# Where the later modulation columns are computed: from attention to the values' stage and retention, with retention's state steps widened and its normed result on ScalarE

## The chip, the cores and the metric

One Trainium2 chip, one of its cores. The metric is the device time of one execution in microseconds (us), the median of the runs shown. The core has a matrix engine (PE, TensorE), three elementwise engines (DVE is VectorE, ACT is ScalarE, POOL is GpSimd), and SP (SyncE), which here only issues DMA transfers. SBUF is the memory of 128 partitions that the engines work on, and PSUM holds PE's results in eight banks of 512 numbers for each partition.

## The reference

A decoder block on 1024 tokens of 1024 channels, all float32. A vector c gives six modulation vectors, `mod = silu(c) @ w_ada + b_ada`: shift, scale and gate of the token mixer (sh1, sc1, g1) and of the MLP (sh2, sc2, g2).

```
h = modulate(rms_norm(x, norm1_g), sh1, sc1)
x = x + g1 * token_mixer(h)
h = modulate(rms_norm(x, norm2_g), sh2, sc2)
x = x + g2 * square(relu(h @ w1)) @ w2
out = rms_norm(x, norm_f_g)
```

The token mixer adds two gated branches. One is retention: 4 heads, 256 channels of queries and keys, 512 of values, in 8 chunks of 128 tokens.

```
s = (q @ k.T) * inner_decay
o = s @ v + (q @ state) * q_decay
state = state * chunk_decay + (k * k_decay).T @ v
```

Each row of o is then normalised (its mean taken off, divided by the root of variance plus 1e-5), scaled, shifted, multiplied by silu(rg) and projected. The other branch is dilated window attention in three groups of four heads, whose results are merged by their softmax denominators.

## The kernel before

Every product of float32 matrices is made of three matmuls on rounded operands: each operand x is split into a high part (a rounded copy, by ScalarE) and a low part (x minus the high part, by DVE), and `mm3` (L199 to L206) adds low times high, high times low and high times high. L202, L204 and L206 are therefore the lines of nearly all matmuls, and L192 and L193 those of the splits of weights (`split_w`).

The stages follow each other in time: attention's values, queries and keys (`queries_keys`), retention's values (`values`), retention (`chunk`, 32 times), attention (`att_step`, `cover_step`, `gate_step`), the output projections, the MLP.

All instructions stand in the order in which the program writes them; each engine works through its own list in that order and waits at an instruction until its operands are there. So the place of a line decides what stands behind it.

`Steps` runs the program as a list of steps, each with its loads and a body. Loads go through one ring (`raw`) of three buffers, issued on SP in the order of the list, never more than three ahead of those used (L85 is the issue). Before a body runs, all loads of the next step are prepared, and those loads at the head of the step after it that are weights. Preparing a weight is its split; preparing queries (`q_prep`, L1210 and L1211) is theirs; preparing a modulation column (`mod_prep`, L453 to L455) is one DVE product with the silu of c (`cb`, broadcast over the partitions) that also sums, and a small addition of the bias. Of the 48 columns of 128 numbers, 16 are made at the start. The other 32 (`later_mods`) are loads of later steps: three in each head of retention (ahead of chunks 2, 5 and 7), and 20 in attention, two for each of ten steps.

**Values.** `values` goes through 14 items (`VSEQ`), each with four parts of 12 matmuls (`v_mm`). Weight loads are issued two items ahead; high and low parts of the next item (`v_w`, `v_low`) are made in parts 0 to 2, results of the part before are handled after each part (`v_post`). The table of cosines, `cs`, was used for the rotations in the stage before, and is not read here.

**Retention.** `chunk(h, c)` writes, in this order: PE's product of keys and values for the new state (kv, two banks), a part of the projection of rg; DVE's update of the state, by 512 columns twice (L700, L702); the preparing of the next step's load (`ahead(2)`); the scores of the next chunk (`s_kt`: sT and kT on PE, then sm, smh, sml, kh, kl on ScalarE and DVE, L636 to L647); o on PE; the high and low parts of the state, by 512 columns twice (L715, L716); the next-but-one chunk's queries (`jit_qk`: j on ScalarE, its low part on POOL); the transposes of the previous chunk's normed result (`on_T`: oT on PE, four copies on ScalarE); the rest of rg; mean and variance of o (L726, L727), gr, the reciprocal root on POOL (L729), a multiply (L730), and the normed result onm on DVE (L732). In four chunks of each head after the first, `u_final` follows: scale and shift on ScalarE (L668, two halves), the product with silu(rg) on DVE (L670), and the store of y. PSUM has, in retention, two pairs of banks (tag mm, `ps_mm`) and four single banks (tag s, `ps_s`).

**Attention.** `att_step` projects one head's keys (ak, 48 matmuls), with the scores of the previous head woven in after two of eight parts; then splits the keys (`k_split`: kh on ScalarE L1219, kl on DVE L1220), and takes maximum and exponential of the previous head's scores (`scores_end`). There are six such steps for each of two pairs of heads. In the first step, POOL's queue is given the sums of y in DRAM (`result_sums`).

Of the kernel before, what the change touches and what calls it, by code (L numbers as in the profile page):

```python
# [40 lines left out]
CS_QD = 132  # L41
CS_QD2 = 136
# [92 lines left out]
def block_kernel(ctx, tc, io, stop=None, dbg=None):  # L135
# [37 lines left out]
    cb = cst.tile([P, 1024], F32, name="cb")  # L173
# [141 lines left out]
    right0 = r0.enter_context(tc.tile_pool(name="right0", bufs=1, side="right"))  # L315

# [355 lines left out]

    def chunk(h, c, ahead, w=None):
# [15 lines left out]
        kvs = []  # L689
        if c < NC - 1:  # L690
            kh, kl = hd["k", g]
            for i in range(2):
                kv = ps_s(f"kv{h}{c}{i}")
                mm3([kv], (kh[:, i, :], kl[:, i, :]), [(vh, vl)], True, True)
                kvs.append(kv)
        if g > 0:
            proj_mm(hd["rgp"], hd["rgw"], ks[:1])
        for i, kv in enumerate(kvs):
            if c == 0:
                nc.vector.tensor_copy(st[:, i, :], kv)  # L700
            else:
                nc.vector.scalar_tensor_tensor(st[:, i, :], st[:, i, :], float(GAMMA[h] ** C), kv,  # L702
                                               op0=ALU.mult, op1=ALU.add)
        ahead(2)
        if g + 1 < NG:
            s_kt(g + 1)
        po = ps_s(f"o{h}{c}")
# [5 lines left out]
        if c < NC - 1:  # L713
            for i in range(2):
                nc.scalar.copy(sh[:, i, :], st[:, i, :])  # L715
                nc.vector.tensor_sub(sl[:, i, :], st[:, i, :], fv(sh[:, i, :]))  # L716
# [11 lines left out]
        nc.vector.tensor_scalar(gr, ba[:, 1:2], ct[:, CS_QD2 + h:CS_QD2 + h + 1], GN_EPS, op0=ALU.mult, op1=ALU.add)  # L728
        nc.gpsimd.tensor_tensor(gr, gr, mhalf[:, 0:1], op=ALU.pow)  # L729
        nc.vector.tensor_mul(gr, gr, ct[:, CS_QD + h:CS_QD + h + 1])  # L730
        on = p.tile([P, DV], F32, tag="on", bufs=1, name=f"onm{h}{c}")
        nc.vector.tensor_scalar(on, po, ba[:, 0:1], gr, op0=ALU.subtract, op1=ALU.mult)  # L732
        hd["o", h, c] = on
# [335 lines left out]

    def values(ahead):  # L1070
# [3 lines left out]
        for i, (hp, n) in enumerate(VSEQ):  # L1074
            if i + 2 <= last:
                v_load(i + 2)
            for p in range(4):
# [8 lines left out]
                if p == 2 and i < last:  # L1086
                    v_low(i + 1, 1)

# [21 lines left out]
    for g in (1, 2):  # L1110
        for kk in range(4):
# [4 lines left out]
    later_mods = [G1 + k for k in range(NK)] + [SH2 + k for k in range(NK)] + \  # L1116
                 [SC2 + k for k in range(NK)] + [G2 + k for k in range(NK)]
# [216 lines left out]
    def weights(pair):  # L1334
# [4 lines left out]
        wt = p.tile([P, 3, 8, 2], F32, tag="wt", name=f"wt{pair}")  # L1339
        wg = p.tile([P, 2, 8, 2], F32, tag="wg", name=f"wg{pair}")  # L1340
# [8 lines left out]
        nc.vector.tensor_add(sm, stn[0][:, :, 2:4], stn[1][:, :, 2:4])  # L1349
        nc.vector.tensor_add(sm, sm, stn[2][:, :, 2:4])  # L1350
# [121 lines left out]
    def att_step(pair, i):  # L1472
# [3 lines left out]
        def body(*args):  # L1476
# [897 lines left out]
def _constants():  # L2374
# [9 lines left out]
    for h in range(H):  # L2384
# [4 lines left out]
        cst[:, CS_QD + h] = np.exp(lg * (i + 1))  # L2389
        cst[:, CS_QD2 + h] = np.exp(2 * lg * (i + 1))  # L2390
# [71 lines left out]
```

## Time and profile before

| | us |
|---|---|
| median of three runs | 2323.57 (2323.11 to 2323.8) |
| the profiled execution | 2327.32 |
| its span, first to last instruction | 2325.5 |
| PE busy | 2198.7 (95%) |
| DVE busy | 1486.2 (64%) |
| ACT busy | 920.8 (40%) |
| POOL busy | 145.2 (6%) |

Times in the trace count from the first instruction. A line of the kernel is named L and its number. In a group row stand the number of instructions, then the engine's busy time in us and the mean of one in ns, then the idle time of the engine just before them and what ended it. In a wait row stand who waited, for whom, the total in us, how often, and the longest. Durations of PE's matmuls overlap: 128 x 512 matmuls start some 0.23 us apart and last 0.39. The granted clock is a share of full speed.

### The profile page before, as it was taken

Reading aid. Unit: us, or ns where it says so; the run is one execution under the profiler, and the core shown is the slowest. Engines: PE = TensorE matmul, PEld = TensorE weight load, DVE = VectorE, ACT = ScalarE, POOL = GpSimd, SP = SyncE. Lnnn points to the kernel's source line nnn. Section 1 sums busy time; section 2 is a strip of 40 time slices with the busy share of each in tenths; the row PEclk is TensorE's granted clock in tenths of the full one; section 3 lists DMA queues with packets and bytes.
Section 4 is the critical chain, followed back from the end, with each engine's and each line's share of the span. In section 5 each row is a group of like instructions: output and inputs, shape, how many; then the busy total and the mean of one; then the engine's idle time right before and its main releaser. Section 6 shows DMA issues by size and latency. Waiting matters only on the chain.

```text
span 2325.5 us, 27170 instructions
## 1 busy us (share of the span) xinstructions
PE 2198.7 (95%) x10082; PEld 1813.7 (78%) x10082; DVE 1486.2 (64%) x2341; ACT 920.8 (40%) x1697; POOL 145.2 (6%) x168
## 2 busy tenths in 40 slices
PE   7999999999999998875989999999989999999998
PEld 5877888888787777764877878888868888788887
DVE  6537777764445888853555564486786665687845
ACT  4423222332343545532543543534454444443412
POOL 0001111000001222200000000001100000000003
PEclk9999999999999999987999999999999999999999
DMA  9548998432477465478433336555224443745322
GB/s 357 204 144 295 280 299 253 155 127 91 181 253 250 158 208 186 159 253 235 143 108 100 110 125 229 208 199 195 95 94 155 150 150 121 290 164 179 118 84 73
DMA packets 156674, 417.30 MB, mean 179 GB/s; under 512 B 27318, under 2 KB 55229, under 8 KB 152126
## 3 DMA queue, kind: packets, MB, share of 16 engines
q1 hardware_dynamic: 150846, 371.53, 45.5%
q0 software_dynamic: 5696, 44.04, 8.0%
q8 instruction: 79, 1.29, 0.2%
q14 instruction: 53, 0.43, 0.1%
HBM read 320.46 MB, written 160.32 MB: 207 GB/s over the span
## 4 chain that ended last, share of the span: by engine, by line
PE 44%; DVE 6%; DMA 4%; ACT 3%; issue 1%; POOL 0%; SPq 0%; POOLq 0%; DVEq 0%; ACTq 0%
PE fp L202 4%; PE fp L204 4%; PE fp L206 4%; DMA raw<-in_w_ak_dram 2%; PE f2a L204 2%; PE f2a L206 2%; PE f2a L202 2%; ACT P L1273 1%; PE wo L202 1%; PE wo L204 1%; PE wo L206 1%; PE roa L206 1%; PE roa L204 1%; PE roa L202 1%; PE ak L202 1%; PE ak L204 1%
## 5 line engine op out<-in xcount | busy, mean ns | idle before, releaser
L202 PE MATMUL qap<-hh,qaw 128*128 128x512 f32 x264 | 102.9, 390 | 3.9 <-ACT qat L281 2.2
L204 PE MATMUL qap<-hl,qaw 128*128 128x512 f32 x264 | 102.7, 389 | 0.0
L206 PE MATMUL qap<-hh,qaw 128*128 128x512 f32 x264 | 102.7, 389 | 0.0
L614 POOL TENSOR_TENSOR j<-qk,j 128x512 fp32r<-128x512 f32 x32 | 43.1, 1348 | 490.9 <-ACT j L613 490.9
L1919 ACT ACTIVATE a<-a 128x512 f32<-128x512 f32 x48 | 30.3, 632 | 78.7 <-DVE a L1918 78.7
L202 PEld LDWEIGHTS qap<-hh,qaw 128*128 128x128 f32 x264 | 49.5, 188 | 15.0 <-ACT qat L281 2.6
L1273 ACT ACTIVATE P<-P,ng 128x128 f32<-128x128 f32 (+1 forms) x96 | 41.9, 438 | 45.1 <-DVE ng L1270 45.1
L202 PE MATMUL sc<-kh,ql 128*128 128x256 f32 (+1 forms) x96 | 28.3, 295 | 33.2 <-ACT kh L1219 33.2
L206 PEld LDWEIGHTS qap<-hh,qaw 128*128 128x128 f32 x264 | 49.5, 188 | 10.3
L204 PEld LDWEIGHTS qap<-hl,qaw 128*128 128x128 f32 x264 | 49.6, 188 | 10.2
L259 DVE TENSOR_TENSOR fw<-w1r,fw 128x512 fp32r<-128x512 f32 x48 | 33.0, 688 | 36.3 <-ACT fw L249 36.3
L1816 POOL TENSOR_TENSOR accnf<-accnf,sqnf 128x256 f32<-128x256 f32 (+1 forms) x18 | 16.6, 921 | 619.9 <-ACT sqnf L1815 619.9
L259 DVE TENSOR_TENSOR qaw<-wa,qaw 128x512 fp32r<-128x512 f32 x66 | 45.1, 687 | 14.9 <-ACT qaw L249 14.5
L2105 ACT CAST w2h<-w2s 128x512 fp32r<-128x512 f32 x36 | 22.4, 621 | 78.0 <-DVE w2s L2143 76.2
L202 PE MATMUL fp<-h2h,fw 128*128 128x512 f32 x128 | 50.0, 391 | 0.0
L1816 POOL TENSOR_TENSOR accn<-accn,sqn 128x512 f32<-128x512 f32 x12 | 15.6, 1297 | 549.8 <-ACT sqn L1815 549.8
L206 PE MATMUL fp<-h2h,fw 128*128 128x512 f32 x128 | 49.8, 389 | 0.0
L204 PE MATMUL fp<-h2l,fw 128*128 128x512 f32 x128 | 49.8, 389 | 0.0
L202 PE MATMUL roa<-rh,rwl 128*128 128x512 f32 x128 | 49.8, 389 | 0.0
L204 PE MATMUL roa<-rl,rwh 128*128 128x512 f32 x128 | 49.8, 389 | 0.0
L206 PE MATMUL roa<-rh,rwh 128*128 128x512 f32 x128 | 49.8, 389 | 0.0
L249 ACT CAST qaw<-wa 128x512 fp32r<-128x512 f32 x66 | 39.7, 617 | 24.9 <-PE qap L206 22.3
(3073 smaller groups left out, 7161.3 us busy)
## 6 DMA issues: line engine op xcount, KB each, us to landing
v<-vd SPq DMA_DIRECT2D x32, 512.0 KB, 4.9
raw<-in_w_ada_dram SPq DMA_DIRECT2D x32, 512.0 KB, 5.4
w1r<-in_w_ff_dram SPq DMA_DIRECT2D x32, 512.0 KB, 4.9
vd<-vo SPq DMA_DIRECT2D x24, 512.0 KB, 6.5
yt<-y POOLq DMA_DIRECT2D x6, 2048.0 KB, 15.5
xsd<-as SPq DMA_DIRECT2D x24, 512.0 KB, 2.7
w2r<-in_w_ff2s_dram SPq DMA_DIRECT2D x24, 512.0 KB, 7.4
em<-in_w_ada_dram SPq DMA_DIRECT2D x16, 512.0 KB, 10.2
```

The source lines that it names most:

```text
L202: nc.tensor.matmul(o, wl, xh, start=first, stop=False, skip_group_check=skip)
L204: nc.tensor.matmul(o, wh, xl, start=False, stop=False, skip_group_check=skip)
L206: nc.tensor.matmul(o, wh, xh, start=False, stop=last, skip_group_check=skip)
L249: nc.scalar.copy(t[:, :512], src)
L259: nc.vector.tensor_sub(t[:, 512:], src, fv(t[:, :512]))
L614: nc.gpsimd.tensor_sub(t[:, 1], src, fv(t[:, 0]))
L1273: nc.scalar.activation(v, v, AF.Exp, bias=ng[:, blk:blk + 1], accum_out=st[:, g, blk, 2 + a:3 + a])
L1816: (nc.vector if f == 7 else nc.gpsimd).tensor_add(G["acc", key], G["acc", key], sq)
L1919: nc.scalar.activation(o, o, AF.Relu)
L2105: nc.scalar.copy(hi, src)
```

## The change

The 32 later columns are given out anew. Thirteen go to the values' stage: at the start of each item but the last, one column's load is issued on SP into one half of `cs`; `v_mod` makes its sum on DVE in the last part of the item after. The other 19 go to retention: five in heads 0 to 2 (ahead of chunks 1, 2, 3, 5 and 6), four in head 3 (1, 3, 5 and 6). Attention's steps have none.

In `chunk`, kv becomes one pair of banks (`ps_mm`) in place of two single ones; the update of the state, its high part and its low part are each one instruction of 1024 columns. The scale by the query decay is folded into eps: gr becomes one addition ahead of POOL's root, and the multiply after it goes. The normed result is no longer made at the end of the chunk by DVE but by `normed(g - 1)` in the next chunk, behind `s_kt` and ahead of o: a small DVE product (nb, minus mean times gr), and one ScalarE instruction with scale and bias over 512 columns. For the last chunk, `normed` is called in attention's first step.

`cb` moves to a pool that closes after retention, and `weights` writes products and their sum to tiles of their own.

```diff
-CS_QD = 132
-CS_QD2 = 136
+CS_EPS = 132
...
-    cb = cst.tile([P, 1024], F32, name="cb")
...
+    cb = right0.tile([P, 1024], F32, name="cb")
...
+    def normed(g):
+
+        h, c = divmod(g, NC)
+        po, ba, gr = hd["o", h, c]
+        nb = R["p"].tile([P, 1], F32, tag="nb", bufs=2, name=f"nb{h}{c}")
+        nc.vector.scalar_tensor_tensor(nb, ba[:, 0:1], -1.0, gr, op0=ALU.mult, op1=ALU.mult)
+        on = R["p"].tile([P, DV], F32, tag="on", bufs=1, name=f"onm{h}{c}")
+        nc.scalar.activation(on, po, AF.Identity, scale=gr, bias=nb)
+        hd["o", h, c] = on
...
-        kvs = []
         if c < NC - 1:
             kh, kl = hd["k", g]
+            kv = ps_mm(f"kv{h}{c}")
             for i in range(2):
-                kv = ps_s(f"kv{h}{c}{i}")
-                mm3([kv], (kh[:, i, :], kl[:, i, :]), [(vh, vl)], True, True)
-                kvs.append(kv)
+                mm3([kv[:, i]], (kh[:, i, :], kl[:, i, :]), [(vh, vl)], True, True)
...
-        for i, kv in enumerate(kvs):
-            if c == 0:
-                nc.vector.tensor_copy(st[:, i, :], kv)
-            else:
-                nc.vector.scalar_tensor_tensor(st[:, i, :], st[:, i, :], float(GAMMA[h] ** C), kv,
-                                               op0=ALU.mult, op1=ALU.add)
+        if c == 0:
+            nc.vector.tensor_copy(flat(st), flat(kv))
+        elif c < NC - 1:
+            nc.vector.scalar_tensor_tensor(flat(st), flat(st), float(GAMMA[h] ** C), flat(kv),
+                                           op0=ALU.mult, op1=ALU.add)
         ahead(2)
         if g + 1 < NG:
             s_kt(g + 1)
+        if g > 0:
+            normed(g - 1)
         po = ps_s(f"o{h}{c}")
...
-            for i in range(2):
-                nc.scalar.copy(sh[:, i, :], st[:, i, :])
-                nc.vector.tensor_sub(sl[:, i, :], st[:, i, :], fv(sh[:, i, :]))
+            nc.scalar.copy(flat(sh), flat(st))
+            nc.vector.tensor_sub(flat(sl), flat(st), fv(flat(sh)))
...
-        nc.vector.tensor_scalar(gr, ba[:, 1:2], ct[:, CS_QD2 + h:CS_QD2 + h + 1], GN_EPS, op0=ALU.mult, op1=ALU.add)
+        nc.vector.tensor_add(gr, ba[:, 1:2], ct[:, CS_EPS + h:CS_EPS + h + 1])
         nc.gpsimd.tensor_tensor(gr, gr, mhalf[:, 0:1], op=ALU.pow)
-        nc.vector.tensor_mul(gr, gr, ct[:, CS_QD + h:CS_QD + h + 1])
-        on = p.tile([P, DV], F32, tag="on", bufs=1, name=f"onm{h}{c}")
-        nc.vector.tensor_scalar(on, po, ba[:, 0:1], gr, op0=ALU.subtract, op1=ALU.mult)
-        hd["o", h, c] = on
+        hd["o", h, c] = po, ba, gr
...
+    def v_mod(i):
+
+        t, j = cs[:, i % 2], VMODS[i]
+        nc.vector.scalar_tensor_tensor(t, t, 1.0, cb, op0=ALU.mult, op1=ALU.mult, accum_out=mods[:, j:j + 1])
+        nc.vector.tensor_add(mods[:, j:j + 1], mods[:, j:j + 1], vec[:, VC_BADA + j:VC_BADA + j + 1])
+
+    VMODS = [later_mods.pop(0) for _ in range(len(VSEQ) - 1)]
...
+            if i < last:
+                nc.sync.dma_start(cs[:, i % 2], io["w_ada"][VMODS[i]])
...
+                if p == 3 and i > 0:
+                    v_mod(i - 1)
...
-                      ([mod_load(later_mods.pop(0))] if c in (2, 5, 7) else []), manual=True)
+                      ([mod_load(later_mods.pop(0))] if c in ((1, 2, 3, 5, 6) if h < 3 else (1, 3, 5, 6)) else []), manual=True)
...
-            nc.vector.tensor_mul(stn[g][:, :, 2:4], wt[:, g], stn[g][:, :, 2:4])
-        sm = mx
+            nc.vector.tensor_mul(pr[:, g], wt[:, g], stn[g][:, :, 2:4])
...
+                normed(NG - 1)
                 on_T(H - 1, NC - 1)
...
-                      ([(aq_d[pair, *combos[i - 1]], q_prep(pair, *combos[i - 1]))] if i > 0 else []) +
-                      [mod_load(later_mods.pop(0)) for _ in range(2 if i > 0 else 0)],
+                      ([(aq_d[pair, *combos[i - 1]], q_prep(pair, *combos[i - 1]))] if i > 0 else []),
...
-        cst[:, CS_QD + h] = np.exp(lg * (i + 1))
-        cst[:, CS_QD2 + h] = np.exp(2 * lg * (i + 1))
+        cst[:, CS_EPS + h] = GN_EPS * np.exp(-2 * lg * (i + 1))
```

More of the change, by code (lines that the diff above doesn't have):

```diff
@@ L1068, in v_post @@
         nc.sync.dma_start(v_d[2 * hp + int(blk[0]) - 1][:, p + 4 * (int(blk[1]) - 1)], fv(t))
+    later_mods = [G1 + k for k in range(NK)] + [SH2 + k for k in range(NK)] + \
+                 [SC2 + k for k in range(NK)] + [G2 + k for k in range(NK)]
+    def v_mod(i):
[3 more added lines that the diff above has]
+    VMODS = [later_mods.pop(0) for _ in range(len(VSEQ) - 1)]
     def values(ahead):
@@ L1339, in weights @@
         wt = p.tile([P, 3, 8, 2], F32, tag="wt", name=f"wt{pair}")
+        pr = p.tile([P, 3, 8, 2], F32, tag="pr", name=f"pr{pair}")
+        sm = p.tile([P, 8, 2], F32, tag="ssum", name=f"ssum{pair}")
         wg = p.tile([P, 2, 8, 2], F32, tag="wg", name=f"wg{pair}")
@@ L1346, in weights @@
         for g in range(3):
[L1347 to L1350 removed]
+            nc.vector.tensor_mul(pr[:, g], wt[:, g], stn[g][:, :, 2:4])
+        nc.vector.tensor_add(sm, pr[:, 0], pr[:, 1])
+        nc.vector.tensor_add(sm, sm, pr[:, 2])
         nc.vector.reciprocal(sm, sm)
```

2 lines of the change are left out of this document (removed).

## The prediction, made before the changed kernel was run

> **What bounds the kernel now.** The page comes first: which engine is full, and in which slices it isn't. Each row is the span in 40 slices of 58 us, busy share or granted clock in tenths.
>
> ```profile
> PE 7999999999999998875989999999989999999998
> PEclk9999999999999999987999999999999999999999
> ```
>
> PE is full except at the ends and in slices 15 to 20 and 29, and two slices lose clock. So a gain can only come from those places, and a loss is made wherever PE gets a new wait. Next, the busy time by stage: values (579 to 742 us), retention (742 to 996), attention (996 to 1387).
>
> ```profile
> core 0: us, PE busy (x) PEld busy (x) DVE busy (x) ACT busy (x) POOL busy (x), PEclk, DMA share, GB/s
> 579.00:742.00 163.00, 159.22 (x705) 131.41 (x704) 75.84 (x91) 62.79 (x90) 7.09 (x10) 1.00 0.64 223
> 742.00:996.00 254.00, 232.09 (x1111) 187.12 (x1110) 207.61 (x444) 125.44 (x339) 57.08 (x61) 0.98 0.54 178
> 996.00:1387.00 391.00, 327.98 (x1698) 277.03 (x1698) 203.80 (x337) 158.52 (x360) 7.47 (x9) 0.91 0.51 155
> ```
>
> PE is idle 3.8 us in values, 21.9 in retention, 63.0 in attention. Attention also has a mean clock of 0.91; retention has DVE busy for 82% of its time. Then PE's own waits (total, times, longest), first attention, then retention.
>
> ```profile
> PE sc L202 <- ACT kh L1219: 33.2, 4, 15.2
> PE sc L204 <- DVE kl L1220: 14.7, 6, 3.0
> PE pv L1408 <- DVE vl L1303: 5.7, 1, 5.7
> ```
>
> ```profile
> PE o L202 <- DVE state L702: 12.9, 17, 1.3
> PE kT L632 <- DVE onm L732: 6.7, 13, 0.9
> ```
>
> The chain of waits tells why kh is late in attention (start, duration, what).
>
> ```profile
> 1012.32 10.05 DMA raw<-aqd
> 1022.40 1.07 ACT qh L1210
> ...
> 1024.74 11.91 DMA raw<-in_w_ak_dram
> 1036.74 1.05 ACT raw_8204h L192
> ...
> 1086.87 10.33 DMA raw<-in_w_ak_dram
> ```
>
> kh is no slow operation. ScalarE works its list in the order in which it is written, and ahead of kh stands the split of a later step's key weights, whose load has not landed. That load is late because the ring has three raw buffers and a step of attention takes four loads: key weights, queries, two modulation columns. A key weight's buffer comes free only when the step before has used its queries (the load starts at 1024.74, just behind the queries), and then it takes 10 to 12 us.
>
> **Attention loses its 20 columns.** A step is left with two loads. With three buffers, the key weights two steps ahead are then issued while this step begins, a whole step (11 us of projection and the scores) before the split. Loads of 10 to 12 us fit. Gone are the 33.2; most of the 14.7, where kl stands behind two columns on DVE; and the 5.7, where vl does: 53.6 at most. With the waits goes clock. 9% of 391 us is 35 us of clock, which is 70 us at half rate; I take half of them as PE's idle time, where a low clock costs nothing, so 17 us are lost by busy PE. Sum 71. What is late next in the first pair of heads is DMA itself, since the result sums run there on POOL's queue. The same view of the stage, cut finer:
>
> ```profile
> 1038.00:1064.00 26.00, 16.21 (x72) 13.25 (x72) 10.14 (x16) 8.07 (x21) 1.71 (x2) 0.83 0.90 271
> 1064.00:1099.00 35.00, 16.78 (x72) 13.95 (x72) 10.08 (x16) 6.72 (x20) 2.82 (x3) 0.70 0.85 244
> ```
>
> I leave 3 us for it: -68. Bounds: -75 (other small waits go too) and -25 (DMA share stays at 0.9, and loads that are issued earlier also land later). I take the end near -71, since ten of the loads in that queue are gone.
>
> **Values get 13 columns.** Each is one 512 KB load on SP's queue into the table of cosines, idle by then, and the DVE product with its sum, read out and added to the bias. The groups of DVE in retention (count | busy, mean ns | idle before) give their price, and that of what goes there:
>
> ```profile
> L732 DVE TENSOR_SCALAR onm<-o,ba,gr 128x512 f32<-128x512 f32 x31 | 25.1, 811 | 3.6 <-PE kv L206 0.5
> ...
> L453 DVE SCALAR_TENSOR_TENSOR raw<-raw,cb 128x1024 f32<-128x1024 f32 x12 | 14.6, 1219 | 0.0
> ...
> L730 DVE TENSOR_TENSOR gr<-gr,ct 128x1 f32<-128x1 f32 x31 | 5.0, 160 | 21.4 <-POOL gr L729 21.4
> L455 DVE TENSOR_TENSOR mods<-mods,vec 128x1 f32<-128x1 f32 x12 | 1.9, 160 | 0.4
> ```
>
> 1.22 + 0.16 = 1.4 us a column, 18 us for 13. DVE has 87 us free in values, and the weights' low parts that PE needs come earlier in each item, so this is covered. The 6.8 MB more in 163 us are 42 GB/s on top of 223, against the 271 above. A load waits on SP for the column two items back; behind it are value stores and weight loads two items ahead, which nobody needs for some 20 us. Only the last column has no cover: it stands ahead of the last post and of chunk 0's scores, where PE waits for DVE already. +1 us (0 to 1.5).
>
> **Retention.** Four edits meet in one loop, so they are priced together. Seven more columns: 10 us on DVE. The wider state, its high part and its low part each become one instruction of 1024 columns, at about the same time as the pair. One DVE multiply of gr goes (0.16, and with it the wait of 21.4 for POOL). onm goes from DVE (0.81) to ScalarE, with a small DVE multiply (nb) ahead. These relieve DVE by 25.1 + 5.0 + 21.4 - some 7 for nb = 45 us. The kv banks become a pair shared with rg; a new rg then waits for the Silu of the old, but stands behind kv's six matmuls on PE, so I put 0 (to 2) on it.
>
> What speaks against it is the place. The new call stands behind all of the next chunk's score work, so nb is behind kl on DVE, the normed result is behind kh on ScalarE, and stateh, j and the copies are behind the normed result. One chunk of before, in order of time:
>
> ```profile
> 759.50 0.22 PE L627 MATMUL sT<-j 128*128 128x128 f32 x1
> 759.76 0.27 ACT L636 COPY sm<-sT 128x128 f32<-128x128 f32 x1 [2.03 <-PE sT L627]
> 760.83 0.50 PE L202 MATMUL o<-stateh,j 128*128 128x512 f32 x1 [0.15 <-DVE state L702]
> 761.29 0.28 DVE L637 TENSOR_TENSOR sm<-sm,sT 128x128 f32<-128x128 f32 x1
> 761.60 0.29 DVE L638 TENSOR_TENSOR sm<-sm,decay 128x128 f32<-128x128 f32 x1
> 761.93 0.30 ACT L639 CAST smh<-sm 128x128 fp32r<-128x128 f32 x1 [1.91 <-DVE sm L638]
> 762.13 0.47 ACT L646 ACTIVATE kh<-kT,ct 128x256 fp32r<-128x256 f32 x1
> 762.64 0.49 DVE L647 SCALAR_TENSOR_TENSOR kl<-kT,ct,kh 128x256 fp32r<-128x256 f32 x1
> 763.01 0.60 PE L657 MATMUL oT<-ct,onm 128*128 128x128 f32 x4
> ```
>
> Now oT has its operand before kl ends. After the change: sT ends at 759.72, the copy is done 0.33 later, add to mul 0.31, mul to smh 0.33, smh to kh 0.20, kh to kl 0.51, kl 0.51, nb 0.25 (an estimate from the 0.16 row and a semaphore), and the normed result. For that the nearest row is the same function with two per-partition operands, same width:
>
> ```profile
> L668 ACT ACTIVATE on<-on,gnt 128x512 f32<-128x512 f32 x24 | 18.6, 842 | 0.0
> ```
>
> Together 3.3 us. PE needs from the end of sT 0.4 for kT and 2.1 for nine matmuls of o, about 2.45. So oT waits **0.85 us in a bare chunk**. A column or a weight split ahead of the add starts it 0.5 later: **1.4**. Chunk 0 of a later head has three matmuls of o, not nine (1.4 less), and a column: **2.8**. In the four chunks after a final step of the head before, the loop through ScalarE and DVE decides:
>
> ```profile
> 807.18 1.13 ACT L715 CAST stateh<-state 128x512 fp32r<-128x512 f32 x2
> ...
> 809.36 1.55 ACT L668 ACTIVATE on<-on,gnt 128x512 f32<-128x512 f32 x2
> ```
>
> ```profile
> 811.84 1.22 DVE L670 TENSOR_TENSOR on<-on,srg 128x1024 f32<-128x1024 f32 x1
> ...
> 815.51 0.28 DVE L637 TENSOR_TENSOR sm<-sm,sT 128x128 f32<-128x128 f32 x1
> ```
>
> Stateh to the end of the final step is 3.7, its product to the add 3.7 (with state and a column), add to the end of kl 1.9, nb and normed 1.05: 10.3 us, for a chunk in which PE has 232.1 / 32 = 7.3 and some start-up. I take a wait of **2.8**.
>
> Sum: 12 x 2.8, 3 x 2.8, 12 x 1.4 (six in head 0, two in each other), 4 x 0.85: 33.6 + 8.4 + 16.8 + 3.4 = 62, less 1.4 for the one such chunk without column or split, and some 6% because rows overlap a little: 57. Before: 21.9. So +35.
>
> Then the clock. Half rate was granted here, after two waits in one stretch; the row behind is the page's for a matmul of the same size at full rate:
>
> ```profile
> 811.98 0.44 PE L632 MATMUL kT<-ct,qk 128*128 128x128 f32 x2 [0.55 <-DVE onm L732]
> 813.71 0.80 PE L202 MATMUL o<-stateh,j 128*128 128x512 f32 x1 [1.29 <-DVE state L702]
> 814.31 0.63 PE L204 MATMUL o<-statel,j 128*128 128x512 f32 x1
> ```
>
> ```profile
> L202 PE MATMUL qap<-hh,qaw 128*128 128x512 f32 x264 | 102.9, 390 | 3.9 <-ACT qat L281 2.2
> ```
>
> 0.63 us where 0.39 is the rule marks half rate. The 0.02 of 254 us are 5 us of clock, three such stretches. A wait of 2.8 is longer than these two together, so I expect some ten stretches; most of the lost 1.7 us each falls where ScalarE and DVE set the pace. +5.
>
> [...]
>
> Retention: **+40**. Bounds: -20 (all its waits vanish, DVE being relieved) and +60 (each of 15 long waits pays 1.7 in full). The middle, because the order of the instructions is fixed and their rows are known.
>
> **The rest** costs nothing: the column vector cb moves to a pool that closes after retention, the softmax weights write to new small tiles with the same instructions, and the scale of eps replaces a multiply-add by an add.
>
> **Sum.** -68 + 1 + 40 = -27. The profiled execution took 2327.3 us (span 2325.5), 3.7 over the median 2323.57; differences hold for both: 2296.6.
>
> **Rivals.**
> - Retention isn't slowed: normed is early enough, DVE's 45 us of relief pay. For: DVE is at 82%, and both waits of PE name it. Against: kl stands ahead of nb. Seven columns +8, waits -15: 2323.6 - 68 - 7 + 1 = 2250.
> - The clock falls in most chunks of retention and lengthens the loop: +20 more, 2317. For: the stretch at 813.7. Against: PE isn't the loop there.
> - Slower: attention's loads stay late. Place: the first pair, DMA share 0.85 to 0.90. If a load that is issued earlier only queues longer behind the sums, the waits of 8 to 15 us stay, and only the second pair's part and the columns' DVE time are won, 25: 2323.6 - 25 + 41 = 2340. It decides once more than 27 of the 68 are not won. Against: the second pair's waits were short with the same four loads, and half the bytes go.
> - The columns were not the cause and the places only swap: 2323, if attention gives 41 and retention takes it.
>
> **How the numbers follow.** Forecast 0.47, retention not slowed 0.17, clock 0.16, loads late 0.14, even 0.06. The measurement tells about 0.2% (4.6 us) from no change. Faster: 0.47 + 0.17 + most of the clock case = 0.77; same 0.07; slower 0.16. The range leaves out the late loads and the better half of the second case: 2258 to 2328; the likeliest case alone has 2282 to 2312.
>
> **What would show it.** Right: in attention, kh no longer heads PE's waits, and idle plus clock give back about 70 us. In retention, oT waits for onm on ScalarE, some 30 times, 50 to 60 us in all, and the waits for state and onm on DVE are gone. Values keep their 163 us. Wrong: oT without waits, or weight loads of 10 us still in the chain of attention.

## The result and the profile after

The changed kernel takes 2300.8 us (median of four runs, 2296.95 to 2302.19), the kernel before beside it 2323.7. The ratio is 0.9898, with a 95% interval of 0.9881 to 0.9915: some 23 us are gained. The profiled execution of the changed kernel took 2296.95 us, with a span of 2295.1; it is the fastest of the four.

The page of the changed kernel, busy share and granted clock of PE in 40 slices:

```profile
PE   7999999999999878889999999999989999999998
PEclk9999999999999999999999999999999999999999
```

The slices of attention (18 to 23, counted from 0) are full now. Those of retention, which stand ahead of them, got emptier. By stage, first before, cut at the same places of the program, then after (length, then busy time and count of PE, PEld, DVE, ACT, POOL; granted clock; DMA share; GB/s; the rows are values, retention, attention and all that follows):

```profile
core 0: us, PE busy (x) PEld busy (x) DVE busy (x) ACT busy (x) POOL busy (x), PEclk, DMA share, GB/s
579.00:740.10 161.10, 157.38 (x697) 129.87 (x695) 74.77 (x88) 62.12 (x88) 7.09 (x10) 1.00 0.63 220
740.10:996.00 255.90, 233.93 (x1117) 188.66 (x1118) 208.68 (x448) 126.11 (x341) 57.08 (x61) 0.98 0.54 180
996.00:1386.00 390.00, 326.98 (x1693) 276.22 (x1693) 203.80 (x337) 157.52 (x359) 7.47 (x9) 0.91 0.51 155
1386.00:2325.50 939.50, 920.18 (x4147) 761.82 (x4145) 634.04 (x906) 386.40 (x602) 36.93 (x35) 0.99 0.45 156
```

```profile
579.00:739.40 160.40, 156.12 (x691) 128.89 (x689) 90.60 (x127) 60.16 (x87) 7.98 (x10) 1.00 0.73 261
739.40:1032.40 293.00, 239.52 (x1117) 189.27 (x1118) 192.22 (x384) 148.12 (x344) 72.13 (x62) 0.96 0.53 173
1032.40:1352.50 320.10, 309.19 (x1693) 263.15 (x1692) 176.62 (x274) 159.24 (x360) 6.91 (x8) 0.99 0.53 155
1352.50:2295.00 942.50, 920.44 (x4147) 761.96 (x4145) 633.70 (x906) 385.35 (x601) 36.90 (x35) 0.99 0.45 156
```

So the change is a trade of two stages. Attention is 69.9 us shorter. Of that, 52.1 are PE's idle time (390.0 - 326.98 = 63.0 before, 320.1 - 309.19 = 10.9 after), and 17.8 are PE's busy time for the same matmuls, which is clock: the mean went from 0.91 to 0.99. Retention is 37.1 us longer: 31.5 of idle time (22.0 before, 53.5 after) and 5.6 of clock. Values keep their length: between the first matmul of this stage and the first of retention's rg projection there are 157.2 us before and 157.8 after. What follows attention is 3 us longer. All experiments below are read by this table: the length of a stage, and which wait fills it.

PE's waits of the changed kernel in retention, and then in attention (total, times, longest):

```profile
PE oT L656 <- ACT onm L679: 49.3, 31, 3.5
PE kv L200 <- DVE kl L646: 3.1, 1, 3.1
PE rg L200 <- DVE sm L636: 2.3, 1, 2.3
PE rg L200 <- ACT srg L740: 1.0, 1, 1.0
```

```profile
PE pv L1425 <- DVE P L1438: 3.4, 4, 0.9
...
PE sc L202 <- DVE kl L1236: 0.8, 2, 0.4
...
PE pv L1425 <- DVE vl L1319: 0.7, 1, 0.7
```

In attention, no wait for kh is left in the list, and that for kl is 0.8 us where it was 14.7. (The wait of rg for sm in the first list is the end of the values' stage: it ends at 739.49, and is 1.7 us long in the kernel before.) In retention one wait has taken the place of nearly all others: the transposes of the normed result wait for ScalarE 31 times, in each chunk but the first, which has none to make. The last chunk of head 0, in order of time, shows how. (A weight's split stands ahead of its scores on DVE, but ends as the copy of the scores does, so it delays nothing here.)

```profile
806.68 0.30 ACT L638 CAST smh<-sm 128x128 fp32r<-128x128 f32 x1 [0.68 <-DVE sm L637]
...
806.88 0.47 ACT L645 ACTIVATE kh<-kT,ct 128x256 fp32r<-128x256 f32 x1
...
807.39 0.48 DVE L646 SCALAR_TENSOR_TENSOR kl<-kT,ct,kh 128x256 fp32r<-128x256 f32 x1
...
807.79 0.15 DVE L677 SCALAR_TENSOR_TENSOR nb<-ba,gr 128x1 f32<-128x1 f32 x1
...
808.03 0.78 ACT L679 ACTIVATE onm<-o,nb,gr 128x512 f32<-128x512 f32 x1 [0.68 <-DVE nb L677]
...
808.86 0.33 PE L656 MATMUL oT<-ct,onm 128*128 128x128 f32 x1 [0.91 <-ACT onm L679]
```

The operands of nb (`ba` and `gr` of the chunk before) are there by then: gr is done at 806.47, and nb starts at 807.79. ScalarE pauses for DVE twice (0.68 us each). Nothing in the data makes nb late. It is late because it is written behind kl.

### The profile page after: what moved, and what is told of

It is laid out like the page before. It is cut to its first block, busy times and chain, and to the rows that moved or that the text cites. A ratio compares the mean times of both kernels' runs of the same rounds, so it can differ in the third digit from the quotient of the medians.

```text
span 2295.1 us, 27058 instructions
## 1 busy us (share of the span) xinstructions
PE 2186.5 (95%) x10082; PEld 1801.3 (78%) x10082; DVE 1458.0 (64%) x2253; ACT 942.7 (41%) x1701; POOL 160.5 (7%) x168
## 3 DMA queue, kind: packets, MB, share of 16 engines
q8 instruction: 79, 1.29, 0.2%
## 4 chain that ended last, share of the span: by engine, by line
PE 78%; DVE 10%; ACT 6%; DMA 4%; issue 2%; SPq 0%; POOL 0%; ACTq 0%; DVEq 0%; POOLq 0%
PE qap L200 6%; PE qap L204 6%; PE qap L202 6%; PE av L768 4%; PE fp L200 4%; PE fp L202 4%; PE fp L204 4%; PE f2a L202 2%; PE f2a L204 2%; PE f2a L200 2%; PE ak L200 2%; PE ak L202 2%; PE ak L204 2%; PE va L202 1%; PE va L204 1%
## 5 line engine op out<-in xcount | busy, mean ns | idle before, releaser
L613 POOL TENSOR_TENSOR j<-qk,j 128x512 fp32r<-128x512 f32 x32 | 55.2, 1725 | 510.1 <-ACT j L612 495.9
L656 PE MATMUL oT<-ct,onm 128*128 128x128 f32 x128 | 20.9, 286 | 49.3 <-ACT onm L679 49.3
L723 DVE TENSOR_TENSOR statel<-state,stateh 128x1024 fp32r<-128x1024 f32 x28 | 34.3, 1225 | 49.9 <-ACT stateh L722 49.9
L656 PEld LDWEIGHTS oT<-ct,onm 128*128 128x128 f32 x128 | 13.5, 141 | 62.8 <-ACT onm L679 62.6
## 6 DMA issues: line engine op xcount, KB each, us to landing
em<-in_w_ada_dram SPq DMA_DIRECT2D x16, 512.0 KB, 10.2
```

Of the source, the lines that this page charges most:

```text
L613: nc.gpsimd.tensor_sub(t[:, 1], src, fv(t[:, 0]))
L656: nc.tensor.transpose(po[:, e, :], on[:, e * P:(e + 1) * P], ident)
L723: nc.vector.tensor_sub(flat(sl), flat(st), fv(flat(sh)))
```

## The experiments

The changed kernel does two things, so the first four kernels take it apart; the next three vary retention and the share of the columns; the last five look at why attention was slow before. Lengths of stages go from first matmul to first matmul, cut as above: before 157.2, 256.1 and 390.0 for values, retention and attention, after 157.8, 293.2 and 320.2.

**The columns alone.** The changed kernel with the old `chunk`:

```diff
-        if g > 0:
-            normed(g - 1)
+        (the body of chunk as it was before)
```

> The 32 columns as after the change (13 in values, 19 in retention, none in attention), retention's chunk as before it. Theory (the columns' loads are what attention waits for; retention pays for the place of the normed result): attention 320 us as after, retention 256 + 8 to 11 us (seven columns of 1.4 us on a DVE that is 82% busy), so 2260 to 2266 us, faster than both kernels. Rival (retention's edits are what lets DVE carry seven more columns): retention at 290 or more as after, 2295 to 2305.

It took 2268.29 us, ratio 0.9764 (0.9749 to 0.9778). Attention is 319.4 us long, retention 265.8:

```profile
PE o L201 <- DVE state L702: 15.0, 18, 1.3
PE kT L632 <- DVE onm L732: 7.5, 16, 0.7
PE kv L201 <- DVE kl L647: 5.1, 4, 2.5
```

Moving the columns is worth 55 us by itself. All of attention's gain is theirs. Seven columns more in retention cost 9.7 us, 1.4 each, which is what one takes on DVE; the old waits for state and onm come back, a little longer, and one for kl is added. The time is 2 us above the expected range; values, with 159.4 us, are 2 longer than before (three other runs with the same stage have 159.4 as well, the changed kernel and one more 157.8).

**Retention's edits alone**, with the columns where they were before.

```diff
-                      ([mod_load(later_mods.pop(0))] if c in ((1, 2, 3, 5, 6) if h < 3 else (1, 3, 5, 6)) else []), manual=True)
+                      ([mod_load(later_mods.pop(0))] if c in (2, 5, 7) else []), manual=True)
         (values and attention's loads as before)
```

> Retention's chunk as after the change, the columns where they were before. Theory: oT waits for the normed result 31 times, 50 us in all; retention goes from 256 to 285 to 290 us, attention stays at 390: 2352 to 2358 us. Rival (the seven columns make retention longer, the edits relieve DVE): retention 240 to 250, 2308 to 2318 us.

It took 2360.13 us, ratio 1.0158 (1.0135 to 1.0181), 37 us more than before and 2 above the expected range. Both stages came out otherwise than expected: retention longer, attention shorter. Stage rows, retention and attention:

```profile
741.40:1034.20 292.80, 243.95 (x1119) 192.83 (x1120) 183.22 (x362) 148.41 (x344) 72.20 (x62) 0.94 0.48 159
1034.20:1412.60 378.40, 326.08 (x1693) 275.45 (x1692) 202.46 (x333) 158.82 (x360) 6.92 (x8) 0.92 0.52 159
```

The edits of `chunk` are a loss of some 37 us of retention on their own, with or without the seven columns. Retention has almost the same length as in the changed kernel, but not in the same way: it idles 48.9 us (292.8 - 243.95) where the other idles 53.5, and loses 4.4 us more to the clock (243.95 against 239.52 us of busy PE). So the columns do add 4.6 us of wait here; that the lengths agree is partly chance. Attention is 11.5 us shorter than before, with nothing new in it but the last chunk's normed result: kh's wait came out at 23.4 us in place of 33.2. So the two profiled executions are only 30 us apart. This stage, which waits for transfers, moved by that much from one program to the next, and a difference of 10 us in it is no proof by itself.

**The normed result earlier.** The changed kernel, with one call moved:

```diff
+        if g > 0:
+            normed(g - 1)
         ahead(2)
         if g + 1 < NG:
             s_kt(g + 1)
-        if g > 0:
-            normed(g - 1)
```

> The changed kernel with the call of normed moved, from behind the next chunk's scores to ahead of the step's loads. Theory (the place costs, not ScalarE's 0.8 us): nb stands right behind the state's update and the normed result ahead of sm, so oT finds it ready; retention 293 to 260 to 268 us, 2268 to 2276 us. Rival (ScalarE in the loop, or the width of 1024, costs): oT waits on, retention within 8 us of 293, 2293 to 2301 us.

It took 2262.39 us, ratio 0.9738 (0.9723 to 0.9752), 38 us less than the changed kernel by the medians. That is 6 us below the expected range. Between the two profiled executions lie 33 us, and 32 of them in retention, which takes 260.9, at the lower end of what was expected. The waits there:

```profile
PE kv L200 <- DVE kl L646: 13.3, 16, 3.1
PE oT L656 <- ACT onm L679: 5.9, 12, 0.6
PE rg L200 <- ACT srg L740: 2.6, 3, 0.9
```

The same instructions on the same engines, one call three lines higher: oT's wait falls from 49.3 to 5.9 us. The place was the cost of these 32 us, and neither the engine nor the width of the state's steps. Against the columns alone (265.8), the edits in this order win 5 us; in the order of the change they lose 27. What is late next is kl, which now stands behind nb.

**The width alone.** The changed kernel with the three state steps in halves again:

```diff
-            nc.scalar.copy(flat(sh), flat(st))
-            nc.vector.tensor_sub(flat(sl), flat(st), fv(flat(sh)))
+            for i in range(2):
+                nc.scalar.copy(sh[:, i, :], st[:, i, :])
+                nc.vector.tensor_sub(sl[:, i, :], st[:, i, :], fv(sh[:, i, :]))
```

(and the update of the state in the same way)

> The changed kernel with only the state's three steps in halves again; the normed result stays on ScalarE behind the next chunk's scores. Theory (the loop goes through the normed result, and the halves only shorten the last piece of it): within 5 us of the changed kernel, 2294 to 2302 us. Rival (the width makes the loss): 2275 or less.

It took 2299.72 us, ratio 0.9899 (0.9875 to 0.9923): no difference from the changed kernel that could be told. oT waits 48.7 us. While the wait for onm sets the pace, the width doesn't matter.

**The normed result on DVE**, at the chunk's end as before, but with the eps folded in (no multiply of gr) and all else as in the change; once with state steps of 1024 columns and once with halves:

```diff
-        hd["o", h, c] = po, ba, gr
+        on = p.tile([P, DV], F32, tag="on", bufs=1, name=f"onm{h}{c}")
+        nc.vector.tensor_scalar(on, po, ba[:, 0:1], gr, op0=ALU.subtract, op1=ALU.mult)
+        hd["o", h, c] = on
```

> The changed kernel with the normed result on DVE at the chunk's end (without gr's multiply), but the state's three steps still 1024 wide. Theory (the place of the normed result was the cost, and the width costs a little, since the low part of 1024 can't start before the whole high part): retention 268 to 274 us, 6 to 12 more than with halves (262.6), 2270 to 2278 us. Rival (the width is free or a gain): 263 or less, 2266 or less.

> The changed kernel with the normed result on DVE at the chunk's end again (without the multiply of gr) and the state's three steps in halves of 512 columns; kv stays in a pair of banks, the columns stay as after. Theory: retention 256 to 261 us although it has seven columns more, since neither o nor kT waits for a bank of DVE's any more; with attention at 320, 2256 to 2262 us, some 6 us faster than with the columns alone. Rival (the pair of banks brings nothing): as the columns alone, 2263 or more.

With the wide steps: 2272.45 us, ratio 0.9781 (0.9761 to 0.9801), retention 269.9, as expected. With halves: 2266.84, ratio 0.9756 (0.9738 to 0.9774), retention 262.6; this time is 5 us above what was expected, and lies where the rival put it. Against the columns alone (265.8), the pair of banks and the folded eps bring 3 us of retention, and no difference of the medians that could be told. The waits, first of the wide version, then of the halves:

```profile
PE kv L200 <- DVE kl L646: 26.0, 21, 3.1
PE rg L200 <- ACT srg L730: 3.2, 2, 2.3
PE sT L624 <- POOL j L613: 2.6, 3, 0.9
```

```profile
PE kv L200 <- DVE kl L646: 23.1, 20, 3.1
PE rg L200 <- ACT srg L732: 5.3, 4, 2.4
...
PE sT L624 <- POOL j L613: 0.5, 2, 0.3
```

What was missed is the new wait: with onm on DVE again, kl is late for kv. Here, where oT no longer waits, the width does cost: 7 us of retention. The waits for kl and for POOL's j are 2.9 and 2.1 us longer with it (that for srg 2.1 shorter), and PE is busy 237.9 us in place of 233.6 for the same matmuls, which is clock (0.97 against 0.98). Why j is late is told below.

**More columns in values.** The version with halves, with two columns for each item of values (26) and six in retention:

```diff
-    VMODS = [later_mods.pop(0) for _ in range(len(VSEQ) - 1)]
+    VMODS = [later_mods.pop(0) for _ in range(2 * (len(VSEQ) - 1))]
...
-                nc.sync.dma_start(cs[:, i % 2], io["w_ada"][VMODS[i]])
+                for j in range(2):
+                    nc.sync.dma_start(cs[:, j], io["w_ada"][VMODS[2 * i + j]])
...
-                if p == 3 and i > 0:
-                    v_mod(i - 1)
+                if p == 3 and i < last:
+                    v_mod(2 * i)
+                    v_mod(2 * i + 1)
...
-if c in ((1, 2, 3, 5, 6) if h < 3 else (1, 3, 5, 6))
+if c in ((2, 5) if h < 3 else ())
```

> The retention of the run with halves and the normed result on DVE (262.6 us there, 23 of them waits of kv for kl), with 26 columns in values, two for each item and both made in its last part, and six in retention. Theory (DVE's columns ahead of the scores are what delays kl): retention 245 to 252 us, values within 3 us of 158, so 2250 to 2257. Rival (values become bound, by 300 GB/s of DMA or by the columns ahead of their posts): values 165 or more, 2262 or more.

It took 2250.72 us, ratio 0.9699 (0.9665 to 0.9733), which beats both kernels: 71 us under the kernel before beside it, and some 50 under the changed kernel by the medians. Values, retention and attention:

```profile
581.80:741.60 159.80, 155.05 (x679) 127.81 (x678) 106.42 (x166) 59.64 (x86) 7.99 (x10) 0.99 0.83 304
741.60:989.10 247.50, 228.18 (x1119) 184.14 (x1120) 199.91 (x400) 125.71 (x341) 57.69 (x62) 0.99 0.52 175
989.10:1307.60 318.50, 307.69 (x1694) 261.90 (x1693) 177.00 (x273) 157.62 (x359) 7.11 (x9) 1.00 0.52 157
```

Thirteen columns leave retention, and it is 15 us shorter; values take them for 2 us, at 304 GB/s (for 0.4 us against the runs that have 159.4 with 13 columns). The wait of kv for kl falls from 23.1 to 13.9 us. A column costs 1.2 us where DVE sets the pace and at most about 0.15 where PE covers it.

**Why attention was slow: the result sums moved.** The prediction puts attention's long loads down to a ring of three buffers, and expects what is left to come from the sums of y on POOL's queue. These five kernels are the kernel before with one thing changed in attention. First, the call that issues the sums, later in the same step:

```diff
-                result_sums()
...
                 drain(at(gen, 4, lambda: v_split(pair, 0)))
+                if pair == 0:
+                    result_sums()
```

> The kernel before with the result sums of POOL's queue moved from attention's first step to the end of its second gate step, some 120 us later. Theory (three buffers for four loads make the key weights late, and the sums make each load take 10 to 12 us): the waits of the first pair of heads fall from 41 us to about the 7 of the second pair, with their share of the clock; attention 390 to 340 to 355, 2273 to 2290 us. Rival (the order of the ring alone, whatever else DMA does): attention 385 or more, 2318 or more.

2320.28 us, ratio 0.9998 (0.9974 to 1.0022), kh's wait 33.5 us: nothing changed. The edit missed its aim, so the run says nothing on the theory. The first sums started at 1012.0 us into the trace all the same (1012.1 in the kernel before): POOL has nothing else to do there, and what ends its idle time of some 15 us is the store of y that the sums read. The next kernel therefore holds them back by an operand: POOL first has to read the last keys of the first pair of heads.

```diff
-                result_sums()
...
             if n == 0:
+                if pair == 0:
+                    hold = A["p"].tile([P, 8], F32, tag="hold", name="hold")
+                    nc.gpsimd.tensor_tensor(hold, fv(A["k", 0, 1][0][:, :8]), mhalf, op=ALU.mult)
+                    result_sums()
                 v_fetch(pair, 1)
```

> The kernel before with the result sums held back for good: a small POOL instruction ahead of them reads the last keys of attention's first pair, so POOL's queue can't issue them before about 1113 us. (Moving only the call changed nothing: POOL has no other work and issued the sums at 1012 us as before.) Theory (late issue through the ring, made long by the sums): loads of key weights in the first pair land in 3 to 5 us, its waits fall from 41 us to 10 to 20, some 5 to 10 come back in the second pair's first steps; attention 350 to 370, 2283 to 2303 us. Rival (the ring alone): the waits of the first pair stay above 33 us, 2315 or more.

2301.85 us, ratio 0.9901 (0.9869 to 0.9933), attention 366.9 us. The tile that the sums are made in (issues; shortest, median and longest issue in ns; first and last start), and the first load of key weights in the chain of waits, first with the call moved, then with the sums held:

```profile
L564 POOL DMA_DIRECT2D yt<-y x2: 601/824/1048, 1012.0 to 1025.5; - x2
...
1026.44 11.63 DMA raw<-in_w_ak_dram
```

```profile
L564 POOL DMA_DIRECT2D yt<-y x2: 601/823/1045, 1094.8 to 1105.3; - x2
...
1018.60 4.94 DMA raw<-in_w_ak_dram
```

So it is the sums that make a load of key weights take 11 us; without them it takes 5. kh's wait falls from 33.2 to 3.6 us. Against that stands a new wait of 10.2 us for P, at 1150 us, where the sums now run. They are the likely cause, though no run tried it: ahead of the wait stand a store and a load of softmax weights of 8 KB each, which take 17.8 and 18.2 us in the median beside the sums, and 7.5 and 2.2 us in the kernel before, where the last sum was issued some 50 us earlier. The stage gains 23 us of the 70 that moving the columns gains.

**Short products.** The columns are still loaded in attention, but only 8 of their 1024 elements are multiplied and summed (this leaves out most of these sums):

```diff
-    nc.vector.scalar_tensor_tensor(raw, raw, 1.0, cb, op0=ALU.mult, op1=ALU.mult, ...
+    nc.vector.scalar_tensor_tensor(raw[:, :8], raw[:, :8], 1.0, cb[:, :8], op0=ALU.mult, op1=ALU.mult, ...
```

> The kernel before; attention's 20 columns are loaded as before, but DVE multiplies and sums only 8 of their 1024 elements, so most of these columns' sum is left out. Theory (the loads in the ring cost, DVE's 27 us are a small part): the waits of sc and pv for DVE's kl and vl (20 us) fall to about a third, those for kh stay; 2305 to 2315 us. Rival (DVE's time for the columns is what delays the queue): most of the 70 us of attention go, 2260 to 2280.

2311.04 us, ratio 0.9955 (0.9933 to 0.9976), attention 376.6; kh's wait 25.6 us, kl's 12.2, vl's 5.5. The time is as expected, the waits are not: those for kl and vl were to fall to a third. DVE's time for the columns is worth 13 us at most, not 70. As an unedited attention moved by 11 us above, even that is not certain; the waits for kl and vl, which hardly changed (14.7 and 5.7 before), are the better witness that the columns' work on DVE doesn't make them. DVE's list in the kernel before shows what does:

```profile
1037.81 1.23 DVE L193 TENSOR_TENSOR raw_8204l<-raw,raw_8204h 128x1024 fp32r<-128x1024 f32 x1 [9.50 <-ACT raw_8204h L192]
...
1040.75 1.22 DVE L1220 TENSOR_TENSOR kl<-ak,kh 128x1024 fp32r<-128x1024 f32 x1
```

DVE is done with the columns 9.5 us ahead of the first row, and then waits for the late key weights too, whose low part stands ahead of kl. So it is in five of the six waits for kl and in the one for vl, 17.4 us in all. Only the first wait for kl (3.0 us) has the two columns straight ahead of it, and that one fell most with the short products, to 0.9.

**Columns ahead of the queries** in the loads of a step:

```diff
-                      ([(aq_d[pair, *combos[i - 1]], q_prep(pair, *combos[i - 1]))] if i > 0 else []) +
-                      [mod_load(later_mods.pop(0)) for _ in range(2 if i > 0 else 0)],
+                      [mod_load(later_mods.pop(0)) for _ in range(2 if i > 0 else 0)] +
+                      ([(aq_d[pair, *combos[i - 1]], q_prep(pair, *combos[i - 1]))] if i > 0 else []),
```

> The kernel before with the two columns ahead of the queries in a step's loads. Bytes and DVE time are the same; the key weights' load starts when the first column is used, and no longer has to wait for the queries' split behind ScalarE's exponentials. Theory (the moment at which the load starts counts): the wait for kh falls from 33 to 15 to 25 us, 2298 to 2315 us. Rival (only the amount of loads counts): within 4 us of the kernel before.

2311.35 us, ratio 0.9962 (0.9945 to 0.9979), attention 373.8; kh's wait 27.6 us, kl's 7.9, and one of 2.1 for ql is new. The time is as expected, but kh's wait fell by much less than that, and 16 us of attention are not far above the 11 by which it moved unedited. The order in the ring is worth little; the number of loads is left.

**One column a step**, and the other ten in values:

```diff
-                      [mod_load(later_mods.pop(0)) for _ in range(2 if i > 0 else 0)],
+                      [mod_load(later_mods.pop(0)) for _ in range(1 if i > 0 else 0)],
```

> The kernel before with one column for each of attention's ten steps in place of two; the other ten are made in values, and retention keeps its twelve. Theory (three buffers against four loads a step): with three loads a step the key weights are issued a whole step ahead, so nearly all of attention's gain is there though half of the columns are left; attention 322 to 335, 2255 to 2270 us. Rival (the amount of loads and of DVE's work): half of the gain, attention 350 to 360, 2283 to 2295 us.

2279.46 us, ratio 0.9813 (0.9789 to 0.9837), attention 344.2 us: 46 of the 70 us for half of the columns, between the two ranges. kh's wait is down to 0.9 us, in spite of the sums. The chain of waits shows what is left:

```profile
1028.12 14.09 DMA raw<-in_w_ak_dram
...
1053.08 14.39 DMA std<-st
1068.00 13.85 DMA raw<-aqd
```

A load of key weights takes 14 us here, longer than before, and still PE's wait for kh is all but gone: the load was issued earlier. The one large wait (9.4 us, for ql) is a store of the softmax statistics that takes 14 us beside the sums, and the queries' load that stands behind it and takes as long.

Read together: both conditions are needed for the wait for kh. The sums make each load long (held back, kh's wait is 3.6), and the ring of three buffers with four loads a step issues the load too late to cover that (three loads a step, kh's wait is 0.9). Which of the two one removes hardly matters for kh; the rest of the 70 us (the waits for kl, vl and ql, and the clock) went only with the second column.

## Why the prediction was right

The forecast of 2297 us is 4 from the median and on the time of the profiled execution; it was made of two large terms, and both stand in size. That they agree this closely is partly luck. The terms below are measured on two profiled executions that lie 30.4 us apart, where the medians lie 22.9 apart: that of the changed kernel has a mean clock of 0.990, its other three runs 0.986 to 0.988, and that of the kernel before took 2327.3 us, more than any of its four timed runs.

**Attention, -68: measured -69.8.** The three waits of 53.6 us became 1.5, all idle time fell by 52.1. The clock was put at 17 us and gave 17.8. The 3 us that were left for DMA in the first pair did not show. The step that such loads fit holds: a load of key weights takes as long as it did, and nobody waits for it. The DMA issues of the first pair, first before, then after (KB each, median us to landing):

```profile
raw<-in_w_ak_dram SPq DMA_DIRECT2D x4, 512.0 KB, 7.8
```

```profile
raw<-in_w_ak_dram SPq DMA_DIRECT2D x4, 512.0 KB, 7.9
```

One reading was wrong: the prediction puts the waits for kl and vl down to the columns' work on DVE. For 17.4 of these 20.4 us, DVE waited for the same late key weights as ScalarE. The sum of 53.6 came out all the same, since late loads of key weights make nearly all of the three waits, and the earlier issue removes them.

**Values, +1: measured +0.6.** DVE took 15.8 us more (74.77 to 90.60) and DMA 41 GB/s more, both covered. The last column, the one piece that the prediction held to be exposed, is no more than this 0.6.

**Retention, +40: measured +37.1.** The prediction gave 57 us of idle time where 53.5 were found, and +5 for the clock where 5.6 were. The mechanism is the one that it names: nb behind kl, the normed result behind kh, 31 waits of oT. They sum to 49.3 us, below the 57 and just under the 50 to 60 that were named as the sign. By kind of chunk, the estimates were mostly a little long. The chunk above has 0.91 where 0.85 was worked out; chunk 0 of a later head 2.6 where 2.8 was; a chunk with a column or a split in head 0 has 0.8 to 1.25 where 1.4 was, and the last but one of each head, which makes no kh and kl, 0.5. The four chunks behind a final step were given 2.8 each, and took 1.2, 2.4, 2.2 and 3.4 in head 1: 9.3 for the four, not 11.2. Against that stand 4.1 us of other waits in the stage (kl and srg), which the sum had at nothing. That the place and not the engine does it was an argument in the prediction, and is shown by the kernel with the call moved up: 5.9 us in place of 49.3.

**The clock: seven half-rate stretches, not ten.** In the changed kernel each stretch is 3.4 us long (3.413 in the trace's records of the granted clock), and here are two of the seven, behind a wait of 3.1 and one of 2.6 us (columns as in the stage table):

```profile
750.60:754.00 3.40, 3.40 (x10) 2.69 (x9) 3.33 (x6) 0.16 (x1) 2.36 (x2) 0.51 0.78 282
818.90:822.30 3.40, 3.40 (x10) 2.62 (x9) 3.12 (x5) 2.19 (x7) 2.34 (x2) 0.50 0.00 0
```

PE is busy through all of each stretch (3.40 of 3.40 us, at a clock of 0.50 or 0.51), so each costs it some 1.7 us, where the prediction let most of that fall beside the pace of ScalarE and DVE. Fewer stretches, each dearer: the two errors offset, and that the clock's +5 came out is luck.

Waits of 2.3, 2.6 (three times), 3.1, 3.4 and 3.5 us were each followed by one such stretch; six of 2.2 to 2.5 us, one of 3.4 and all shorter ones were not. The place in time tells them apart. The stretches start at 740.40, 750.64, 818.90, 859.87, 894.00, 934.96 and 969.09 us: the later ones lie 3, 23, 35, 45, 57 and 67 times 3.413 us behind the first, on one grid. Of each wait that cost clock, at least 2.1 us fall into the one interval of this grid that ends where the stretch starts. The wait of 3.4 us that cost none (1004.96 to 1008.38) lies across a boundary, 1.7 us on either side, and of the six others no interval holds more than 1.9. In the kernel before, two short waits within one interval sufficed three times, with 1.8 us together, so the idle time of an interval is not the whole rule.

Five of the seven stretches came after one wait of 2.3 to 3.1 us, and in the row of before two waits of 1.84 us in all (0.55 and 1.29) had been enough. The prediction took that row as its measure and rightly let waits of this length cost clock, though not each of them did.

**The rest, 0: measured +3.1.** One wait of 1.4 us is new (the first matmul of an output projection, for a product of DVE), and one of the MLP's matmuls for a low part (f2a for b21l) grew from 0.2 to 1.7. What makes them late was not shown; they were not in the sum.

**The rivals.** Retention not slowed: the edits alone cost 37 us, so the 45 us by which DVE is relieved bought nothing in this order; with the call moved up, they pay 5. The clock in most chunks: seven stretches, no. Loads that stay late: their duration stayed, as this rival supposed, but the earlier issue hid it. Places that only swap: excluded by the columns alone, at 55 us of gain.

## What to carry to other kernels

On engines that work through a list in order, the place of an instruction in the list can cost more than the instruction (here one call moved by three lines was worth 32 us of retention): ask what stands ahead of it that it doesn't need, before moving it to another engine. A load that is late has two handles, its duration and its moment of issue (kh's wait of 33.2 us fell to 3.6 by the first and to 0.9 by the second), and a ring that is one load a step too shallow can turn a slow transfer into a wait. Small independent work belongs into the stage where the bounding engine covers it (here the matmuls of values: at most about 0.15 us a column, against 1.2 in retention), and moving a call on an engine that has nothing else to do moved nothing here (the first sums started at 1012.0 us, and at 1012.1 before): it took an operand to hold the transfer back.

## What the hardware showed that was not expected

POOL's subtraction that makes the low part of j got slower, though nothing in it was changed. The tile's rows of the kernel before, of the changed kernel, and of the changed kernel with state steps in halves (shortest, median and longest in ns):

```profile
L614 POOL TENSOR_TENSOR j<-qk,j x32: 1285/1357/1465, 720.9 to 983.3; 128x512 fp32r<-128x512 f32 x32
```

```profile
L613 POOL TENSOR_TENSOR j<-qk,j x32: 1290/1754/2270, 720.5 to 1018.6; 128x512 fp32r<-128x512 f32 x32
```

```profile
L613 POOL TENSOR_TENSOR j<-qk,j x32: 1290/1304/2277, 723.0 to 1025.8; 128x512 fp32r<-128x512 f32 x32
```

The width of the state's steps (two on DVE, one on ScalarE) is the only difference between the last two, and the median goes from 1754 to 1304 ns. In the pair with onm on DVE it is the same (1804 with wide steps, 1357 with halves), and there PE's wait for j is 2.6 us against 0.5. A POOL instruction of one column shows that DVE is in it, since it takes 543 ns in the median. Four times in the changed kernel it started 0.22 us behind the start of a DVE subtraction, and took 1393 to 1404 ns each time (the other 28 took 538 to 579). The first:

```profile
804.86 1.21 DVE L191 TENSOR_TENSOR raw_5699l<-raw,raw_5699h 128x1024 fp32r<-128x1024 f32 x1
805.08 1.39 POOL L736 TENSOR_TENSOR gr<-gr,ct 128x1 f32<-128x1 f32 x1 [0.16 <-DVE gr L735]
```

It ended at 806.47, 0.40 us after DVE was done at 806.07, which is less than the 543 ns that it takes in the median; the other three ended 0.40 us after their subtractions too. So POOL's instruction was late beside DVE's, and the wide steps of the state go with a longer j. By what means the one holds up the other, no run here shows, nor the opposite order, a DVE instruction that is held up so by POOL.
